# DeltaNet's small products placed side by side in row and column groups of the array

## The chip, the cores and the metric

The kernel runs on one core of one Trainium2 chip, as one program. The metric is the device time of one execution in microseconds (us); less is better. The engines are named as the profile names them: PE is the matrix engine TensorE (PEld its weight loads), DVE is VectorE, ACT is ScalarE, POOL is GpSimd, and SP is the engine whose queue issues the DMAs. All matrix results land in PSUM, in banks of 128 x 512 f32.

## The reference, cut to what matters

One layer of a hybrid encoder block over 1024 positions of 1024 channels: a gated DeltaNet branch (mixer A), a banded attention branch (mixer B), two gates, an output projection, and a feed-forward part with a short convolution. The change touches mixer A alone, and there the following:

```python
h = rmsnorm(x, norm_mix_w)                       # (1024, 1024)
proj = h @ w_in                                  # q, k, v, z, beta logits, decay logits, ...
...
qa = l2norm(qa)                                  # q / sqrt(sum of squares over the 128 channels of a head + EPS)
beta = sigmoid(ba)                               # 4 heads: 4 beta logits and
g = -exp(a_log) * softplus(aa + dt_bias)         # 4 decay logits for every position
# chunks of 64 positions, 4 heads; per chunk and head:
a_mat = beta * (k @ k.T) * dec_strict            # 64 x 64, strictly lower triangular
sol = triangular_solve(a_mat + eye, rhs)         # unit lower triangular
...
oa = rmsnorm(oa, gdn_norm_w) * silu(z)
```

## The kernel before, in words

Positions stand along the free dimension: BH and BL hold the high and the low part of the input (times the norm's weight) as fp32r, 128 channels by 1024 positions in 8 blocks k. A projection of 128 columns over one half (512 positions) is 24 matmuls of 128x512 in proj_half (L118): for each k high by high, high by low, low by high. The row factor of the RMSNorm, rb, is multiplied in afterwards on VectorE (tile u for the convolutions, gt for the gates).

The order of work is the scheduler's: the kernel is written as a program, every instruction has a priority from its place in it, and the scheduler fixes the order on each engine beforehand by a cost model; the engines then run their queues in that order and wait on semaphores. Two things steer it: `tc.high_priority(offset=PRI)` pulls the recurrent part of a head forward, and `behind()` (L54) puts instructions behind the last matmul traced. The lists C1 to APK at the top of the file say after which step of the fill each part of a head starts. The loop at L662 goes over the heads: while the chain of head h runs (gdn_chain, 16 dependent steps), the projections of the heads to come and of the gates fill TensorE.

What the change and the prediction's steps touch:

- first_split (L208) loads the transposed input in four quarters xT (two for each half of the positions, 4 blocks k each) and makes BH and BL of them. The quarters share the buffers of the tag "WQ", of which there are three, with the tiles WQ of the heads.
- first_rms (L224) loads the rows of x and builds rb through a product of ones with a diagonal (psrb).
- ba_half (L285) computes the 8 logits (4 beta, 4 decay) of one half: wba2 holds the 8 columns of the weight as a high and a low part in 16 of 32 columns, and 16 fp32r matmuls (8 blocks by BH and BL) of 32 columns add up in 32 partitions of the tile psba. baf takes them times rb, and decays (L295) turns them with the constant matrix fold, which adds the high and the low part.
- gdn_solve (L520) inverts the 32x32 diagonal blocks on VectorE, stores them (dZ) and loads them into the block diagonal of zt by four DMAs on SP. gdn_apply (L533) then makes the 32x32 block below the diagonal for each 64-position chunk: a transpose on VectorE, a product nL by zt (tile psB1, "psB" in the profile), a copy to B1 on ScalarE, a product with the transposed block (tile psZ21, "psZ"), a copy into zt. This is written for e = 0 and then for e = 1, the two chunks of each of the 8 blocks of 128 positions; e = 0 reads partitions 32 to 63 and writes 0 to 31 in the first product, e = 1 reads 96 to 127 and writes 64 to 95. The products psW and psU, which start the chain, read zt.
- gdn_qnorm (L605) squares q (sqq) and sums over the 128 channels: eight matmuls with sqq as weights (128x128) and a column of ones as the moving operand, handed to proj_half through the list side, one after each k. gdn_qnorm2 (L614) copies the sums to sx by two copies of 64x8, with the two chunks of a block exchanged. gdn_rms (L622) uses sx at L629 (adding EPS and scaling) and L631, for the norm of the head's output.

Of the kernel before, what the change touches and what calls it, by code (L numbers as in the profile page):

```python
# [8 lines left out]
F32 = mybir.dt.float32  # L9
F32R = mybir.dt.float32r  # L10
AF = mybir.ActivationFunctionType
ALU = mybir.AluOpType
# [4 lines left out]
P = 128  # L17
D = 1024
KT = D // P
T = 1024  # L20
NT = T // P
HN = 512
CH = 64
# [23 lines left out]
def hybrid_kernel(ctx: ExitStack, tc: tile.TileContext, a):  # L47
    nc = tc.nc
    last = {}

    def mm(*args, **kw):
        last["mm"] = nc.tensor.matmul(*args, **kw).ins  # L52
# [6 lines left out]
    cst = ctx.enter_context(tc.tile_pool(name="cst", bufs=1))  # L59
# [7 lines left out]
    BH = big.tile([P, KT, T], F32R, name="BH")  # L67
    BL = big.tile([P, KT, T], F32R, name="BL")
# [1 line left out]
    ident = cst.tile([P, P], F32, name="ident")  # L70
    mhalf = cst.tile([P, 16], F32, name="mhalf")
    nc.vector.memset(mhalf, -0.5)
    ones = cst.tile([P, 1], F32, name="ones")
    nc.vector.memset(ones, 1.0)

    def rsqrt(out, in_):
        n = in_.shape[-1]
# [37 lines left out]
    side = []  # L115
# [45 lines left out]
    psc = psy.enter_context(tc.tile_pool(name="psc", bufs=3, space=PSUM))  # L161
# [32 lines left out]
    gp = gx.enter_context(tc.tile_pool(name="gp", bufs=1, reuse_waits="tile"))  # L194
    gc = gx.enter_context(tc.tile_pool(name="gc", bufs=1, reuse_waits="tile"))
    gd = gx.enter_context(tc.tile_pool(name="gd", bufs=2, space=DRAM))


    ones2 = gc.tile([P, P], F32, name="ones2")
# [3 lines left out]
    nw = prm[:, 49:57]  # L203

    rb = cst.tile([P, T], F32, name="rb")
    ws = []

    def first_split(e, step, wk=None):  # L208

        s = slice(e * HN, (e + 1) * HN)  # L210
        for q in range(2):
            xT = gp.tile([P, 4, HN], F32, tag="WQ", name="xT", bufs=3)
            for j in range(4):
                k = 4 * q + j
                if wk and k in wk:
                    first_w(k, wk[k])
                if j % step == 0:
                    nc.sync.dma_start(xT[:, j:j + step, :],
                                      a["xT"][k * P:(k + step) * P, s].rearrange("(k p) t -> p k t", p=P))
                nc.scalar.activation(BH[:, k, s], xT[:, j, :], AF.Copy, scale=nw[:, k:k + 1])  # L220
                nc.vector.scalar_tensor_tensor(out=BL[:, k, s], in0=xT[:, j, :], scalar=nw[:, k:k + 1],  # L221
                                               in1=BH.bitcast(F32)[:, k, s], op0=ALU.mult, op1=ALU.subtract)
# [32 lines left out]
    nc.sync.dma_start(ident, a["consts"][:, 0:P])  # L255
    first_rms(0)
    wba = prm[:, 65:129].rearrange("p (k c) -> p k c", c=8)
    wba2 = gp.tile([P, KT, 32], F32R, tag="mb", name="wba2")
    nc.vector.memset(wba2.bitcast(F32), 0.0)
    nc.vector.tensor_copy(wba2[:, :, 0:8], wba)  # L260
    nc.vector.tensor_tensor(out=wba2[:, :, 8:16], in0=wba, in1=wba2.bitcast(F32)[:, :, 0:8], op=ALU.subtract)
    cw = prm[:, 0:48].rearrange("p (t j) -> p t j", j=4)
    nc.vector.tensor_scalar_mul(prm[:, 0:49], prm[:, 0:49], 0.5)
    gnw = prm[:, 48:49]
# [18 lines left out]
    baf = gp.tile([P, T], F32, tag="zs", name="baf")  # L283

    def ba_half(e):  # L285
        s = slice(e * HN, (e + 1) * HN)
        psb = psc.tile([P, HN], F32, tag="c", name="psba")
        for k in range(KT):
            mm(psb[0:32], wba2[:, k, :], BH[:, k, s], start=k == 0, stop=False)
            mm(psb[0:32], wba2[:, k, :], BL[:, k, s], start=False, stop=k == KT - 1)  # L290
        nc.vector.tensor_mul(baf[0:32, s], psb[0:32], rb[0:32, s])

    fold = gc.tile([32, 8], F32, name="fold")
    nc.sync.dma_start(fold, a["fold"])
    def decays():  # L295
        psg = psa.tile([P, HN], F32, tag="a", name="psbat")
        for p in range(NT):
            mm(psg[:, p * 8:(p + 1) * 8], baf[0:32, p * P:(p + 1) * P], fold, start=True, stop=True)
        bav = psg[:, 0:64].rearrange("p (n c) -> p n c", c=8)

        beta = gc.tile([P, NT, GH], F32, name="beta")
# [231 lines left out]
    def gdn_apply(c):  # L533
        nL, zt = c["nL"], zts[0]
        Z11 = gp.tile([P, NT, 32], F32, tag="Z11", name="Z11")
        psx1 = psa.tile([P, HN], F32, tag="a", name="psB1")
        B1 = gp.tile([P, NT, 32], F32, tag="B1", name="B1")
        psx2 = psa.tile([P, HN], F32, tag="a", name="psZ21")
        for e in range(2):
            r0 = slice(e * CH, e * CH + 32)  # L540
            r1 = slice(e * CH + 32, (e + 1) * CH)
            nc.vector.transpose(out=Z11[r0], in_=zt[r0, :, r0])
            for p in range(NT):
                mm(psx1[r0, p * 32:(p + 1) * 32], nL[r1, p, 0:32], zt[r1, p, r1], start=True, stop=True)
            nc.scalar.copy(B1[r0].rearrange("p n j -> p (n j)"), psx1[r0, 0:256])
            for p in range(NT):
                mm(psx2[r0, p * 32:(p + 1) * 32], Z11[r0, p, :], B1[r0, p, :], start=True, stop=True)
            nc.scalar.copy(zt[r0, :, r1], psx2[r0, 0:256].rearrange("p (n j) -> p n j", j=32))

        WQ, nKs, Vs = c["WQ"], c["nKs"], c["Vs"]  # L550
        U = gp.tile([P, NT, P], F32, tag="U", name="U")
        for q in range(2):
            n = slice(4 * q, 4 * q + 4)
            psW = psa.tile([P, HN], F32, tag="a", name="psW")
            for i in range(4):
                mm(psW[:, i * P:(i + 1) * P], nKs[:, 4 * q + i, :], zt[:, 4 * q + i, :], start=True, stop=True)
            w4 = psW.rearrange("p (n e i) -> p n e i", e=2, i=CH)
            for e in range(2):
                nc.scalar.copy(WQ[:, n, e * 192:e * 192 + CH], w4[:, :, e, :])
            psU = psa.tile([P, HN], F32, tag="a", name="psU")  # L560
            for i in range(4):
                mm(psU[:, i * P:(i + 1) * P], zt[:, 4 * q + i, :], Vs[:, 4 * q + i, :], start=True, stop=True)
            nc.scalar.copy(U[:, n, :], psU.rearrange("p (n d) -> p n d", d=P))
        c["U"] = U
# [40 lines left out]
    def gdn_qnorm(c):  # L605

        sqq = gp.tile([P, NT, P], F32, tag="zs", name="sqq")
        nc.scalar.activation(sqq, c["WQ"][:, :, 64:192], AF.Square)
        psn = psc.tile([P, 8], F32, tag="c", name="psn")
        for p in range(NT):  # L610
            side.append(lambda p=p: mm(psn[:, p:p + 1], sqq[:, p, :], ones, start=True, stop=True))
        c["psn"] = psn

    def gdn_qnorm2(c):  # L614

        psn = c["psn"]
        sx = gp.tile([P, NT], F32, tag="sx", name="sx", bufs=2)
        for e in range(2):
            nc.scalar.copy(sx[(1 - e) * CH:(2 - e) * CH], psn[e * CH:(e + 1) * CH])
        c["sx"] = sx  # L620

    def gdn_rms(c):  # L622
# [39 lines left out]
    for h in range(-1, GH):  # L662
# [35 lines left out]
        n = 0  # L698
# [229 lines left out]
    c = {}  # L928
# [825 lines left out]
def layout(inp):  # L1754
# [6 lines left out]
    def col_tiles(w):  # L1761
# [33 lines left out]
    r["consts"] = np.concatenate(  # L1795
        [np.eye(P), le, le[:, (i + CH) % P], gt, half, ~half, (i % CH)[:, None] <= j[None, :],
         (i % CH)[:, None] > j[None, :], e8], axis=1).astype(np.float32)
    r["fold"] = np.concatenate([np.eye(8), np.eye(8), np.zeros((16, 8))], axis=0).astype(np.float32)
    return r


# [12 lines left out]
```

## Time and profile before

| what | value |
|---|---|
| time, median of 3 runs | 1572.11 us |
| the runs | 1569.9, 1572.11, 1572.12 us |
| span of the profiled execution | 1571.7 us |
| granted TensorE clock, mean | 0.997 |
| PE busy, share of the span | 1520.5 us, 97% |
| PEld busy | 1246.0 us, 79% |
| DVE busy | 1122.3 us, 71% |
| ACT busy | 715.4 us, 46% |
| POOL busy | 597.3 us, 38% |

The span runs from the first to the last instruction of one execution under the profiler; its own time is the span and what little lies around it, and the median of the runs stands 0.4 us above the span. Busy times of an engine add up what it was occupied with; matmuls overlap, so the distance between the starts of two matmuls says more of their cost than their duration. In a row of the timeline the first number is the start in us, the second the time in us of the row, which may cover several instructions (xN), then engine, line, operation, output<-inputs, for matmuls rows*columns of the weights and the shape of the moving operand, and in brackets how long the engine had stood idle and what ended that. Most matmuls come through one helper and bear its line, L52, so they are told apart by tile. In the views of waits the numbers after the colon are us in all, times, and the longest. In the table by stretch the columns are the stretch, its length, busy us and instructions of PE, PEld, DVE, ACT and POOL, the granted clock, and the DMAs' share and GB/s.

### The profile page before, as it was taken

The page shows a single profiled execution, that of the slowest core. Times are in us where ns is not written, and L with a number is a line of the kernel's source. Part 1 is how long each engine was busy: PE and PEld are TensorE (multiplying, and loading weights), DVE is VectorE, ACT ScalarE, POOL GpSimd, SP SyncE. Part 2 cuts the span into 40 slices and gives each one's busy share as a digit, 9 for nine tenths or more (in the row PEclk, how much of TensorE's full clock was granted, in tenths as well). Part 3 has the DMA queues.
Part 4 walks back from the last instruction along what each step waited for, and adds up shares of the span by engine and source line. Part 5 has one row for each costly group of instructions (what it writes and reads, how often), then busy time and mean ns, then how long its engine had stood idle before and what let it go on. Part 6 is the DMA issues. An engine that isn't in the chain of part 4 may idle for free.

```text
span 1571.7 us, 21185 instructions
## 1 busy us (share of the span) xinstructions
PE 1520.5 (97%) x7687; PEld 1246.0 (79%) x7687; DVE 1122.3 (71%) x2146; ACT 715.4 (46%) x1408; POOL 597.3 (38%) x455
## 2 busy tenths in 40 slices
PE   8999999999999999999999999999999999999997
PEld 6778777886777788787887888888888888788875
DVE  7885867948536878866664567777777777786886
ACT  7644526363225656654222345444444443433344
POOL 3522223212131101110220259877777775323253
PEclk9999999999999999999999999999999999999998
DMA  8112131122131101113553213323223232775523
GB/s 297 40 45 88 44 101 31 54 78 68 61 125 49 36 23 57 30 61 119 171 180 109 94 67 107 122 101 101 101 101 101 101 101 98 264 233 162 180 81 141
DMA packets 74505, 162.03 MB, mean 103 GB/s; under 512 B 15649, under 2 KB 16929, under 8 KB 74401
## 3 DMA queue, kind: packets, MB, share of 16 engines
q1 hardware_dynamic: 74400, 160.68, 30.8%
q8 instruction: 60, 0.98, 0.2%
q14 instruction: 45, 0.36, 0.1%
HBM read 120.55 MB, written 40.11 MB: 102 GB/s over the span
## 4 chain that ended last, share of the span: by engine, by line
PE 49%; DVE 3%; issue 2%; DMA 1%; ACT 1%; SPq 1%; POOL 0%; POOLq 0%; DVEq 0%; ACTq 0%
PE psph L52 8%; PE pb L52 7%; PE psd L52 6%; PE psout L52 5%; PE pa L52 5%; PE pc L52 5%; PE pb L1151 4%; PE psd L1506 3%; PE pa L1151 2%; PE pc L1151 2%; DVE wdl L1165 1%; DVE yu L1165 1%; PE pso L52 1%; SPq L1165 1%; DMA araw<-dA 1%
## 5 line engine op out<-in xcount | busy, mean ns | idle before, releaser
L82 POOL TENSOR_TENSOR wlo<-wraw,whi 128x1024 fp32r<-128x1024 f32 (+1 forms) x57 | 120.0, 2106 | 477.8 <-ACT whi L81 288.1
L52 PE MATMUL psph<-BH,whi 128*128 128x512 f32 x688 | 280.7, 408 | 10.5 <-ACT BH L220 5.2
L52 PE MATMUL psph<-BL,whi 128*128 128x512 f32 x688 | 275.6, 401 | 1.2 <-DVE BL L221 1.2
L52 PE MATMUL psph<-BH,wlo 128*128 128x512 f32 x688 | 275.3, 400 | 0.0
L52 PEld LDWEIGHTS psph<-BH,whi 128*128 128x128 f32 x688 | 130.6, 190 | 33.4 <-ACT BH L220 5.4
L1165 POOL TENSOR_TENSOR ol<-wraw,oh 128x512 fp32r<-128x512 f32 x110 | 150.4, 1385 | 6.6 <-ACT oh L1165 6.5
L52 PEld LDWEIGHTS psph<-BL,whi 128*128 128x128 f32 x688 | 130.7, 190 | 22.9 <-DVE BL L221 2.2
L52 PEld LDWEIGHTS psph<-BH,wlo 128*128 128x128 f32 x688 | 130.4, 190 | 22.9
L52 PE MATMUL psd<-wdl,ah 128*128 128x512 f32 (+1 forms) x311 | 121.9, 392 | 5.3 <-DVE wdl L1165 5.3
L1165 POOL TENSOR_TENSOR al<-araw,ah 128x1024 fp32r<-128x1024 f32 (+1 forms) x28 | 68.3, 2441 | 145.8 <-ACT ah L1165 145.7
L52 PE MATMUL psd<-wdh,ah 128*128 128x512 f32 (+1 forms) x311 | 120.2, 390 | 1.5 <-ACT wdh L1165 1.5
L1506 PE MATMUL psd<-wdh,al 128*128 128x512 f32 (+1 forms) x311 | 121.0, 389 | 0.0
L1165 POOL TENSOR_TENSOR wraw<-wraw 128x512 f32<-128x512 f32 x86 | 119.1, 1385 | 4.9
L1165 ACT CAST oh<-wraw 128x512 fp32r<-128x512 f32 x110 | 67.8, 619 | 103.5 <-POOL wraw L1165 103.3
L1165 DVE TENSOR_TENSOR wdl<-W,wdh 128x512 fp32r<-128x512 f32 x77 | 86.6, 1163 | 27.9 <-ACT wdh L1165 27.9
L1165 ACT CAST ah<-araw 128x1024 fp32r<-128x1024 f32 (+1 forms) x39 | 40.6, 1040 | 113.0 <-PE psd L52 57.8
L81 ACT CAST whi<-wraw 128x1024 fp32r<-128x1024 f32 (+2 forms) x61 | 55.3, 907 | 73.0 <-PE psph L52 50.3
L1165 POOL TENSOR_TENSOR gl<-wraw,gh 128x512 fp32r<-128x512 f32 x42 | 56.2, 1340 | 68.6 <-ACT gh L1165 68.6
L52 PEld LDWEIGHTS psd<-wdl,ah 128*128 128x128 f32 x311 | 58.7, 189 | 19.8 <-DVE wdl L1165 8.0
L52 PEld LDWEIGHTS psd<-wdh,ah 128*128 128x128 f32 x311 | 58.8, 189 | 14.1 <-ACT wdh L1165 1.9
L1151 PE MATMUL pa<-BH,gh 128*128 128x512 f32 x176 | 68.6, 390 | 0.0
L52 PE MATMUL pa<-BH,gl 128*128 128x512 f32 x176 | 68.5, 389 | 0.0
(343 smaller groups left out, 3851.0 us busy)
## 6 DMA issues: line engine op xcount, KB each, us to landing
wraw<-w_up SPq DMA_DIRECT2D x44, 512.0 KB, 5.1
wraw<-w_tiles SPq DMA_DIRECT2D x42, 512.0 KB, 3.5
araw<-dA SPq DMA_DIRECT2D x77, 256.0 KB, 3.0
dA<-yu SPq DMA_DIRECT2D x33, 512.0 KB, 3.1
W<-w_down SPq DMA_DIRECT2D x44, 256.0 KB, 4.9
xt<-x SPq DMA_DIRECT2D x16, 512.0 KB, 5.1
dG<-gt SPq DMA_DIRECT2D x16, 512.0 KB, 2.9
ta<-dG SPq DMA_DIRECT2D x16, 256.0 KB, 2.8
```

The costliest lines, as they stand in the source:

```text
L52: last["mm"] = nc.tensor.matmul(*args, **kw).ins
L81: nc.scalar.copy(hi, src)
L82: (eng or nc.gpsimd).tensor_tensor(out=lo, in0=src, in1=hi.bitcast(F32), op=ALU.subtract)
L1151: i = nc.tensor.matmul(ps, wh[:, k], xh[:, k], start=start and k == 0, stop=False, **kw)
L1165: return lambda *args, **kw: tc.keep_in_program_order(f(*args, **kw))
L1506: i = nc.tensor.matmul(ps, al[:, j, ts], wh[:, es], start=False, stop=stop, **kw)
```

## The change

Three groups of small products are placed in different row and column groups of the 128x128 array, and what they need is arranged for it.

- Logits: the 8 blocks k are multiplied in f32 straight from xT, whose quarters are kept in a list (xTs), by the weight times the norm's weight (wba2, f32, 8 of 32 columns used). Block k = 4q + j goes to the 32 partitions j of psba, so four column groups hold four partial sums, over two rounds q. fold is now 128x8 and adds the four.
- Solve: the loops over e and p in gdn_apply are exchanged, so that the products of e = 0 and e = 1, which use different row groups and column groups, alternate; both copies to B1 follow the first 16 products, both copies to zt the second.
- Norm sums: ones (32 columns of ones2) are now the weights and sqq the moving operand, 256 columns for each of four matmuls, each in a column group of its own. All four are handed out at once. gdn_qnorm2 copies the result (tile sn, in the buffer of B1), stores four of its rows to DRAM (dN) and loads sx from there in two DMAs with pieces of one element.

```diff
--- before.py
+++ after.py
@@ -70,8 +70,6 @@
     ident = cst.tile([P, P], F32, name="ident")
     mhalf = cst.tile([P, 16], F32, name="mhalf")
     nc.vector.memset(mhalf, -0.5)
-    ones = cst.tile([P, 1], F32, name="ones")
-    nc.vector.memset(ones, 1.0)
 
     def rsqrt(out, in_):
         n = in_.shape[-1]
@@ -205,11 +203,14 @@
     rb = cst.tile([P, T], F32, name="rb")
     ws = []
 
+    xTs = ([], [])
+
     def first_split(e, step, wk=None):
 
         s = slice(e * HN, (e + 1) * HN)
         for q in range(2):
-            xT = gp.tile([P, 4, HN], F32, tag="WQ", name="xT", bufs=3)
+            xTs[e].append(gp.tile([P, 4, HN], F32, tag="WQ", name="xT", bufs=3))
+            xT = xTs[e][-1]
             for j in range(4):
                 k = 4 * q + j
                 if wk and k in wk:
@@ -255,10 +256,9 @@
     nc.sync.dma_start(ident, a["consts"][:, 0:P])
     first_rms(0)
     wba = prm[:, 65:129].rearrange("p (k c) -> p k c", c=8)
-    wba2 = gp.tile([P, KT, 32], F32R, tag="mb", name="wba2")
-    nc.vector.memset(wba2.bitcast(F32), 0.0)
-    nc.vector.tensor_copy(wba2[:, :, 0:8], wba)
-    nc.vector.tensor_tensor(out=wba2[:, :, 8:16], in0=wba, in1=wba2.bitcast(F32)[:, :, 0:8], op=ALU.subtract)
+    wba2 = gp.tile([P, KT, 32], F32, tag="mb", name="wba2")
+    nc.vector.memset(wba2, 0.0)
+    nc.vector.tensor_tensor(out=wba2[:, :, 0:8], in0=wba, in1=nw.unsqueeze(2).broadcast_to([P, KT, 8]), op=ALU.mult)
     cw = prm[:, 0:48].rearrange("p (t j) -> p t j", j=4)
     nc.vector.tensor_scalar_mul(prm[:, 0:49], prm[:, 0:49], 0.5)
     gnw = prm[:, 48:49]
@@ -285,17 +285,18 @@
     def ba_half(e):
         s = slice(e * HN, (e + 1) * HN)
         psb = psc.tile([P, HN], F32, tag="c", name="psba")
-        for k in range(KT):
-            mm(psb[0:32], wba2[:, k, :], BH[:, k, s], start=k == 0, stop=False)
-            mm(psb[0:32], wba2[:, k, :], BL[:, k, s], start=False, stop=k == KT - 1)
-        nc.vector.tensor_mul(baf[0:32, s], psb[0:32], rb[0:32, s])
-
-    fold = gc.tile([32, 8], F32, name="fold")
+        for q in range(2):
+            for j in range(4):
+                mm(psb[j * 32:(j + 1) * 32], wba2[:, 4 * q + j, :], xTs[e][q][:, j, :], start=q == 0, stop=q == 1,
+                   skip_group_check=True)
+        nc.vector.tensor_mul(baf[:, s], psb, rb[:, s])
+
+    fold = gc.tile([P, 8], F32, name="fold")
     nc.sync.dma_start(fold, a["fold"])
     def decays():
         psg = psa.tile([P, HN], F32, tag="a", name="psbat")
         for p in range(NT):
-            mm(psg[:, p * 8:(p + 1) * 8], baf[0:32, p * P:(p + 1) * P], fold, start=True, stop=True)
+            mm(psg[:, p * 8:(p + 1) * 8], baf[:, p * P:(p + 1) * P], fold, start=True, stop=True)
         bav = psg[:, 0:64].rearrange("p (n c) -> p n c", c=8)
 
         beta = gc.tile([P, NT, GH], F32, name="beta")
@@ -536,15 +537,18 @@
         psx1 = psa.tile([P, HN], F32, tag="a", name="psB1")
         B1 = gp.tile([P, NT, 32], F32, tag="B1", name="B1")
         psx2 = psa.tile([P, HN], F32, tag="a", name="psZ21")
-        for e in range(2):
-            r0 = slice(e * CH, e * CH + 32)
-            r1 = slice(e * CH + 32, (e + 1) * CH)
+        rr = [(slice(e * CH, e * CH + 32), slice(e * CH + 32, (e + 1) * CH)) for e in range(2)]
+        for r0, r1 in rr:
             nc.vector.transpose(out=Z11[r0], in_=zt[r0, :, r0])
-            for p in range(NT):
+        for p in range(NT):
+            for r0, r1 in rr:
                 mm(psx1[r0, p * 32:(p + 1) * 32], nL[r1, p, 0:32], zt[r1, p, r1], start=True, stop=True)
+        for r0, r1 in rr:
             nc.scalar.copy(B1[r0].rearrange("p n j -> p (n j)"), psx1[r0, 0:256])
-            for p in range(NT):
+        for p in range(NT):
+            for r0, r1 in rr:
                 mm(psx2[r0, p * 32:(p + 1) * 32], Z11[r0, p, :], B1[r0, p, :], start=True, stop=True)
+        for r0, r1 in rr:
             nc.scalar.copy(zt[r0, :, r1], psx2[r0, 0:256].rearrange("p (n j) -> p n j", j=32))
 
         WQ, nKs, Vs = c["WQ"], c["nKs"], c["Vs"]
@@ -606,17 +610,26 @@
 
         sqq = gp.tile([P, NT, P], F32, tag="zs", name="sqq")
         nc.scalar.activation(sqq, c["WQ"][:, :, 64:192], AF.Square)
-        psn = psc.tile([P, 8], F32, tag="c", name="psn")
-        for p in range(NT):
-            side.append(lambda p=p: mm(psn[:, p:p + 1], sqq[:, p, :], ones, start=True, stop=True))
+        psn = psc.tile([P, 256], F32, tag="c", name="psn")
+
+        def sums():
+            for j in range(4):
+                mm(psn[j * 32:(j + 1) * 32], ones2[:, 0:32], sqq[:, 2 * j:2 * j + 2, :].rearrange("p n t -> p (n t)"),
+                   start=True, stop=True)
+
+        side.append(sums)
         c["psn"] = psn
 
     def gdn_qnorm2(c):
 
-        psn = c["psn"]
+        sn = gp.tile([P, 256], F32, tag="B1", name="sn")
+        nc.scalar.copy(sn, c["psn"])
+        dN = gd.tile([4, 256], F32, tag="dN", name="dN")
+        nc.sync.dma_start(dN, sn[0:P:32, :])
         sx = gp.tile([P, NT], F32, tag="sx", name="sx", bufs=2)
         for e in range(2):
-            nc.scalar.copy(sx[(1 - e) * CH:(2 - e) * CH], psn[e * CH:(e + 1) * CH])
+            nc.sync.dma_start(sx[(1 - e) * CH:(2 - e) * CH, :],
+                              bass.AP(tensor=dN.tensor, offset=dN.offset + e * CH, ap=[[1, CH], [P, NT]]))
         c["sx"] = sx
 
     def gdn_rms(c):
@@ -1795,7 +1808,7 @@
     r["consts"] = np.concatenate(
         [np.eye(P), le, le[:, (i + CH) % P], gt, half, ~half, (i % CH)[:, None] <= j[None, :],
          (i % CH)[:, None] > j[None, :], e8], axis=1).astype(np.float32)
-    r["fold"] = np.concatenate([np.eye(8), np.eye(8), np.zeros((16, 8))], axis=0).astype(np.float32)
+    r["fold"] = np.tile(np.concatenate([np.eye(8), np.zeros((24, 8))], axis=0), (4, 1)).astype(np.float32)
     return r
 
 
```

## The prediction

> **What bounds the kernel now.** I read the page's busy table first, then the 40 slices, then the idle time of TensorE by releaser in the first 420 us, which hold every line that the change touches, and then the busy time of each engine in stretches of that part.
>
> ```profile
> PE 1520.5 (97%) x7687; PEld 1246.0 (79%) x7687; DVE 1122.3 (71%) x2146; ACT 715.4 (46%) x1408; POOL 597.3 (38%) x455
> ...
> PE   8999999999999999999999999999999999999997
> ...
> PE pss L52 <- DVE U L579: 7.3, 6, 1.6
> PE psph L52 <- ACT BH L220: 5.2, 1, 5.2
> PE psph L52 <- DVE gt L171: 3.1, 3, 1.8
> PE psph L52 <- DVE u L381: 1.0, 1, 1.0
> ...
> 25.00:55.00 30.00, 29.85 (x142) 23.41 (x141) 28.15 (x45) 18.18 (x32) 9.66 (x14) 1.00 0.51 178
> 84.00:125.00 41.00, 37.99 (x173) 30.71 (x172) 37.54 (x87) 12.36 (x20) 8.75 (x8) 1.00 0.20 65
> 125.00:230.00 105.00, 102.74 (x624) 83.31 (x623) 72.72 (x179) 47.59 (x119) 27.79 (x27) 1.00 0.22 67
> ```
>
> TensorE is fed without a break: one start-up wait of 5.2 us, then a handful of waits of 1 to 2 us, nearly all on VectorE. So an instruction taken off TensorE is worth the time by which it holds up its successor, unless VectorE (third pair of columns in the stretches: 28.15 of 30 us, 37.54 of 41, later 72.72 of 105) cannot follow. Busy times are no use for this, because matmuls overlap (a 390 ns matmul starts every 0.23 us). I price by distances between starts, on the timeline of TensorE:
>
> ```profile
> 15.94 0.39 PE L52 MATMUL psba<-BH,wba 128*32 128x512 f32 x1
> ...
> 18.95 0.40 PE L52 MATMUL psba<-BL,wba 128*32 128x512 f32 x1
> ...
> 41.61 0.39 PE L52 MATMUL psph<-BH,whi 128*128 128x512 f32 x1
> ...
> 46.83 0.39 PE L52 MATMUL psph<-BH,wlo 128*128 128x512 f32 x1
> ...
> 73.23 1.10 PE L52 MATMUL psQ<-WQ,kf 128*64 128x64 f32 x32
> 74.26 0.50 PE L52 MATMUL psph<-BH,whi 128*128 128x512 f32 x1
> ...
> 102.68 0.39 PE L52 MATMUL psph<-BH,wlo 128*128 128x512 f32 x1
> 102.90 0.28 PE L52 MATMUL psn<-ones,sqq 128*128 128x1 f32 x2
> ...
> 103.59 0.39 PE L52 MATMUL psph<-BH,wlo 128*128 128x512 f32 x1
> ...
> 130.34 0.39 PE L52 MATMUL psph<-BH,wlo 128*128 128x512 f32 x1
> 130.66 0.69 PE L52 MATMUL psB<-zt,nL 32*32 32x32 f32 x16
> 131.27 0.50 PE L52 MATMUL psph<-BH,whi 128*128 128x512 f32 x1
> 131.61 0.40 PE L52 MATMUL psph<-BL,whi 128*128 128x512 f32 x1
> ...
> 132.57 0.21 PE L52 MATMUL psB<-zt,nL 32*32 32x32 f32 x1
> 132.60 0.19 PE L52 MATMUL psZ<-B,Z 32*32 32x32 f32 x1
> 132.62 0.19 PE L52 MATMUL psB<-zt,nL 32*32 32x32 f32 x1
> 132.63 0.19 PE L52 MATMUL psZ<-B,Z 32*32 32x32 f32 x1
> 132.66 0.19 PE L52 MATMUL psB<-zt,nL 32*32 32x32 f32 x1
> ...
> 135.03 0.40 PE L52 MATMUL psph<-BL,whi 128*128 128x512 f32 x1
> 135.27 0.39 PE L52 MATMUL psph<-BH,wlo 128*128 128x512 f32 x1
> 135.49 1.05 PE L52 MATMUL psW<-zt,nKs 128*128 128x128 f32 x8
> 136.38 0.83 PE L52 MATMUL psU<-Vs,zt 128*128 128x128 f32 x6
> ```
>
> A plain projection matmul costs (46.83 - 41.61) / 23 steps = 0.227 us, one of the logits (18.95 - 15.94) / 13 = 0.232. An f32 matmul is two instructions in the trace. With 128 columns each instruction takes (136.38 - 135.49) / 8 = 0.111. The psQ products sit in two column groups of the array by turns and go at (74.26 - 73.23) / 32 = 0.032 with 64-column weights and 64 moving columns, where half of 0.111 would be 0.056: two groups already run side by side. The 32x32 products of one group go at (131.27 - 130.66) / 16 = 0.038; where psB and psZ, in different row and column groups, happen to alternate, four steps take 132.66 - 132.57 = 0.09, so 0.022 each at most. Going into such a burst costs 0.32 - 0.23 = 0.09 over a plain start and coming out 0.34 - 0.23 = 0.11: 0.2 a burst.
>
> **The change part by part.** *Logits.* Before, 32 matmuls at 0.232: 7.4 us, 3.7 a half. After, each half has 8 f32 matmuls over 512 columns, two for each of four column groups. No row shows an f32 matmul that wide. The bounds for one instruction are 0.227 (the 512-column row) and 4 x 0.111 = 0.444 (psW scaled); I take 0.444, the row of the same type. Side by side, a group has 4 instructions: 4 x 0.444 + 0.2 = 2.0 a half, a gain of 1.7. One after another it would be 16 x 0.444 + 0.2 = 7.3, a loss of 3.6 a half. With 0.227 and side by side it would be 1.1, a gain of 2.6. I take side by side, by psQ. But in the first half some of the 8 may be strewn singly between projections, as its first logits are now, and each then costs 0.9 alone; I count 0.9 for that half: 0.9 + 1.7 = 2.6. The sum over the four groups rides on the fold product, whose weights still have 128 columns: nothing. Splitting wba into two parts becomes one multiplication, 0.2 us of VectorE less. The baf product has 128 lanes in place of 32 with the same 512 columns: nothing.
>
> *xT kept longer.* The fourth xT quarter takes the buffer of the first, and its loads now wait for the first round of logits as well as for ScalarE and VectorE.
>
> ```profile
> 17.20 2.31 SPq L218 DMA_DIRECT2D xT<-xT  x4
> 21.33 10.86 SPq L231 DMA_DIRECT2D xt<-x  x4
> ...
> 30.70 1.05 ACT L233 ACTIVATE xt<-xt 128x1024 f32<-128x1024 f32 x1
> ```
>
> The queue comes to these loads only at 17.2 + 2 x 0.58 = 18.4. The first round, from 15.9 on, ends by about 16.9: 1.5 us of cover. Behind them on SP stand the x rows of the second half, the constants, fold and the weights; the x rows are first read at 30.70, so a few us more would still be covered. Nothing.
>
> *Norm sums.* Before, a group of three projections with a psn takes 103.59 - 102.68 = 0.91, so psn costs 0.91 - 3 x 0.227 = 0.23, eight times: 1.84 a head. After, four matmuls over 256 columns in four column groups: 2 x 0.222 + 0.2 = 0.64, a gain of 1.2 a head, 4.8 in all. One after another it is 8 x 0.222 + 0.2 = 2.0, a loss of 0.15 a head; at half the price a gain of 1.4. I take 1.2 on the same ground. Then the sums go through memory: one ScalarE copy of 256 columns in place of two small ones, one store, two loads of 4-byte pieces, all on SP.
>
> ```profile
> L619 ACT COPY sx<-psn x8: 157/160/163, 110.8 to 398.0; 64x8 f32<-64x8 f32 x8
> L548 ACT COPY zt<-psZ x8: 362/362/363, 132.9 to 407.1; 32x256 f32<-32x256 f32 x8
> ...
> dZ<-Zt SPq DMA_DIRECT2D x4, 128.0 KB, 1.7
> zt<-dZ SPq DMA_DIRECT2D x16, 32.0 KB, 2.1
> ...
> DVE Z L542 <- DMA zt<-dZ: 15.7, 7, 4.7
> SPq L87 <- POOL wlo L82: 207.5, 19, 24.8
> ```
>
> The copy is 0.36 for 0.32. The nearest transfer is the solve's own trip, 1.7 and then 2.1 us; the 4-byte loads can hardly be quicker and may be several us slower. Their reader is the EPS step on VectorE (L629), which the scheduler puts into VectorE's order as soon as it believes sx there (L629 follows L619 at once), with solve steps, conv taps and gate products of projections behind it. When VectorE waits for zt in the same way (15.7 us in 7 waits, 4.7 at most), TensorE has its two projection banks, 24 x 0.227 = 5.4 us each, and none of its waits listed above is put down to zt. I count nothing; without that cover it would be about 2.2 us a head, 9 in all. SP waits for each store to land before the next load goes; weights queued behind have a second buffer.
>
> *Solve blocks.* From 130.34 to 135.03 a head starts 8 projection matmuls (131.85, 133.19, 133.52, 133.75 and 134.70 lie between the quoted ones) and both blocks: 4.69 - 8 x 0.227 = 2.87. After, two bursts of 32 instructions at 0.018 to 0.022, say 0.6, plus 0.2: 1.6. Gain 1.3 a head, 5.2 in all; without overlap between groups 2 x (32 x 0.038 + 0.2) = 2.8 and a gain of nothing. psZ now waits for two copies of 0.36 on ScalarE in place of one; projections of 0.227 stand ready to fill in.
>
> **The sum.** 2.6 + 4.8 + 5.2 = 12.6 us less on TensorE. VectorE takes part of it back: logits and head 0's sums (3.8) fall ahead of the stretch 84 to 125, where VectorE is busy 92% and TensorE already waits for gt and u; I give up half, 1.9. Of the other 8.8, won where VectorE is busy 70%, a tenth: 0.9. Left: 9.8. The profiled execution has a span of 1571.7 us; the runs' median is 1572.1, so what lies around the span is 0.4. 1572.1 - 9.8 = 1562.
>
> **A rule against it.** The TensorE time of psQ says that weight loads of two column groups are hidden too: 0.032 a step is less than 0.056, though both groups use all rows. The Trainium skill (TensorE: Matmul & The Clock Gate, Part 3, The mechanism) has it that a weight load overlaps running matmuls only where the row groups differ. The trace disagrees with this for psQ, as far as 64-column loads show; the logits and the norm sums use all rows as well. That is rival B.
>
> **The rivals.** *B: weight loads of groups that share rows are not hidden.* 32 columns cost 0.111 / 4 = 0.028; 32 loads for the logits and 32 for the norm sums are 1.8 us: 1564. Against it stands psQ.
>
> *C: wide f32 operands do not run side by side*, since each group streams 512 or 256 columns of its own from 128 rows, which no row shows. Logits -7.3, norm sums -0.6, solve +4.7: 1572.1 + 3.2 = 1575. For it: psQ streams only 64 columns and proves two groups, not four. It decides against the change once the groups run less than about 1.5 side by side.
>
> *D: VectorE is the bound*, and the freed time returns as waits for gt, u, U and S. If all of the first 3.8 and half of the 8.8 goes, and waits for sx take 2 more, 2.4 are left: 1570. For it: 92% in 84 to 125. Against: VectorE itself waits for TensorE elsewhere.
>
> *E: slower, by sx.* If its loads queue on SP behind a weight load that waits for POOL (207.5 / 19 = 10.9 us on average), VectorE stands at L629 that long, TensorE outlasts 5.4 of it, and four heads lose 4 x 5.5 = 22: 1572.1 - 9.8 + 22 = 1584. It decides from 5.4 + 9.8 / 4 = 7.9 us a head. Against: zt goes through the same queue with 4.7 at most.
>
> **How the numbers follow.** Forecast 0.62, B 0.07, C 0.08, D 0.16, E 0.07. What can be told from no change is 0.2%, 3.1 us. Faster: the forecast, B and a quarter of D, 0.73. Same: the rest of D and some of C, 0.14. Slower: E and most of C, 0.13. The range starts at 1555 (forecast with 0.227 an instruction, 1.8 more on the logits and 0.8 on the sums, and nothing given back to VectorE, 2.8, with a little for a shorter chain) and ends at 1571 with D inside; C and E stay out.
>
> **What would show it.** Logits: 8 f32 matmuls a half in about 2 us; 7 us is C. psn: starts of four matmuls nearly together, some 0.6 a head. psB and psZ: 32 instructions in 0.6 and no second pair of bursts. L629: a wait on sx under 5 us. TensorE's waits for VectorE before 130 us: up by 2 us, not by 4. Wrong it would be through C's single file, through a wait on sx of 8 us or more, or through a new order of instructions that moves waits elsewhere.

## The result, and the profile after

The changed kernel takes 1589.58 us (median of 4 runs, 1587.73 to 1593.38) against 1571.01 us before (4 runs, 1569.78 to 1572.12) on the same chip: a ratio of 1.0115, 95% interval 1.0102 to 1.0129. It is 18.6 us slower; the forecast was 10 us faster. The profiled execution has a span of 1591.6 us (time 1593.4), with a mean granted clock of 0.990, where the execution before showed 0.997. Of all runs below one stands apart: a run of logits_solve took 1886.3 us at a mean clock of 0.751, and is left out of its ratio.

The three edits do on TensorE what the forecast said. The lines are rows of its timeline after: the logits of the second half, one head's norm sums, and (from the run with the solve alone, because both bursts are whole there) the solve's blocks:

```profile
35.84 0.40 PE L52 MATMUL psph<-BH,wlo 128*128 128x512 f32 x1
36.16 1.92 PE L52 MATMUL psba<-xT,wba 128*32 128x512 f32 x14
38.01 0.50 PE L52 MATMUL psph<-BH,whi 128*128 128x512 f32 x1
...
112.69 0.39 PE L52 MATMUL psph<-BH,wlo 128*128 128x512 f32 x1
113.01 0.64 PE L52 MATMUL psn<-sqq,ones 128*32 128x256 f32 x8
113.58 0.50 PE L52 MATMUL psph<-BH,whi 128*128 128x512 f32 x1
```

```profile
133.33 0.69 PE L52 MATMUL psB<-zt,nL 32*32 32x32 f32 x32
133.95 0.50 PE L52 MATMUL psph<-BH,whi 128*128 128x512 f32 x1
...
134.84 0.71 PE L52 MATMUL psZ<-B,Z 32*32 32x32 f32 x32
135.49 0.50 PE L52 MATMUL psph<-BH,whi 128*128 128x512 f32 x1
...
136.52 0.72 PE L52 MATMUL psW<-zt,nKs 128*128 128x128 f32 x5
```

From the projection ahead to the projection behind, less one plain start of 0.227, the logits take 38.01 - 35.84 - 0.23 = 1.94 us (3.7 before), the norm sums 113.58 - 112.69 - 0.23 = 0.66 (1.84 before). A head's solve goes from its first psB to psW in 136.52 - 133.33 = 3.19, where it was 135.49 - 130.66 = 4.83; but 9 projection matmuls started in between before and 7 do now. Without them it is 4.83 - 9 x 0.227 = 2.79 and 3.19 - 7 x 0.227 = 1.60, a gain of 1.2. That is 1.8 + 4 x 1.18 + 4 x 1.2 = 11 us gone from TensorE's own work (the first half's logits come in split bursts and are left out of this sum). The loss is elsewhere, in two places.

The first is VectorE's work in head 0. Busy time by stretch (PE, PEld, DVE, ACT, POOL; the row "sum" covers 60 to 130 us), first before, then after:

```profile
82.00:90.00 8.00, 8.00 (x37) 6.47 (x35) 4.35 (x6) 4.58 (x11) 2.77 (x3) 1.00 0.23 70
...
sum 70.00, PE 65.60 PEld 53.63 DVE 56.48 ACT 34.11 POOL 25.69; mean PE 21.87 PEld 17.88 DVE 18.83 ACT 11.37 POOL 8.56
```

```profile
82.00:90.00 8.00, 8.00 (x37) 6.61 (x36) 0.35 (x2) 7.82 (x23) 0.00 (x0) 1.00 0.31 82
...
sum 70.00, PE 59.95 PEld 48.39 DVE 48.65 ACT 32.62 POOL 22.87; mean PE 19.98 PEld 16.13 DVE 16.22 ACT 10.87 POOL 7.62
```

and the waits in this part of the kernel, first VectorE's for Lr before, then those of VectorE and TensorE after (us in all, times, longest):

```profile
DVE tmp L516 <- DMA Lr<-dL: 0.9, 1, 0.9
```

```profile
DVE u L382 <- PE psph L52: 7.8, 3, 4.2
DVE tmp L517 <- DMA Lr<-dL: 6.9, 1, 6.9
...
PE psph L52 <- DVE u L382: 7.4, 1, 7.4
...
PE psdec L52 <- issue: 1.8, 1, 1.8
```

VectorE stands 6.9 us at the first solve step (L517, L516 before) until Lr has landed, with conv taps queued behind it; between 82 and 90 us it works 0.35 us, and from 60 to 130 us it does 48.65 us of work instead of 56.48. Then TensorE stands 7.4 us for u. The longest such wait before was 1.0 for u.

The second place is where nothing was edited. Two rows of TensorE's timeline in the last stage, 33 starts apart before and 31 after:

```profile
1439.67 0.39 PE L52 MATMUL psd<-wdh,ah 128*128 128x512 f32 x1
...
1447.15 0.39 PE L52 MATMUL psd<-wdh,ah 128*128 128x512 f32 x1
```

```profile
1439.81 0.40 PE L52 MATMUL psd<-wdl,ah 128*128 128x512 f32 x1
...
1447.05 0.39 PE L1519 MATMUL psd<-wdh,al 128*128 128x512 f32 x1
```

The same matmul starts every 7.48 / 33 = 0.227 us before and every 7.24 / 31 = 0.234 after, at a granted clock of 1.0 in both.

### The profile page after: what moved, and what is told of

It reads as the page before. It is cut to its first block, busy times and chain, and to the rows that moved or that the text cites. A ratio compares the mean times of both kernels' runs of the same rounds, so it can differ in the third digit from the quotient of the medians.

```text
span 1591.6 us, 21137 instructions
## 1 busy us (share of the span) xinstructions
PE 1532.5 (96%) x7655; PEld 1238.7 (78%) x7655; DVE 1136.8 (71%) x2144; ACT 712.7 (45%) x1404; POOL 597.2 (38%) x455
## 4 chain that ended last, share of the span: by engine, by line
PE 49%; DVE 4%; issue 2%; DMA 1%; ACT 1%; SPq 1%; POOL 0%; POOLq 0%; DVEq 0%; ACTq 0%
PE psph L52 8%; PE pb L52 7%; PE psd L52 6%; PE psout L52 5%; PE pa L52 5%; PE pc L52 5%; PE pb L1164 4%; PE psd L1519 3%; PE pc L1164 2%; PE pa L1164 2%; DVE wdl L1178 1%; DVE yu L1178 1%; SPq L1178 1%; PE pso L52 1%; DMA araw<-dA 1%
## 5 line engine op out<-in xcount | busy, mean ns | idle before, releaser
L1178 POOL TENSOR_TENSOR ol<-wraw,oh 128x512 fp32r<-128x512 f32 x110 | 157.8, 1451 | 6.6 <-ACT oh L1178 6.5
L1178 POOL TENSOR_TENSOR wraw<-wraw 128x512 f32<-128x512 f32 x86 | 111.9, 1302 | 4.9
L1519 PEld LDWEIGHTS psd<-wdh,al 128*128 128x128 f32 x311 | 58.7, 189 | 13.8
```

The lines of the kernel that those rows point to most:

```text
L1178: return lambda *args, **kw: tc.keep_in_program_order(f(*args, **kw))
L1519: i = nc.tensor.matmul(ps, al[:, j, ts], wh[:, es], start=False, stop=stop, **kw)
```

## Experiments on the late stages: 32 bytes

The change deletes the tile `ones` ([128, 1] f32, for which 32 bytes of every partition are set aside). Everything that is allocated after it from the left side of SBUF moves down by 32 bytes; tiles on the right side (the transposed states XT1 to XT3, the weights wdh and wdl) stay. The psd matmuls above read the weights wdh and wdl, from the right, and ah or al, from the left. My theory A was that operands which then lie differently make matmuls slow; rival O was that only order, clock and transfers differ. Three runs keep the order of all engines and move bytes. Each was timed beside the kernel before, 1571.6 us.

**pad_back**: the changed kernel and

```diff
+    ones = cst.tile([P, 1], F32, name="ones")
+    nc.vector.memset(ones, 1.0)
```

> The changed kernel with the 32-byte tile `ones` allocated and set again, read by nobody. Order of instructions on every engine as in the changed kernel. Theory A (addresses): without that tile everything allocated from the left lies 32 bytes lower, tiles on the right side don't, and matmuls whose two operands then differ by 32 modulo 64 start every 233 to 235 ns instead of 227. The lag of the changed kernel grows from 5.5 us at 460 us to 19.9 at the end, 14 us; with the tile back these 14 go and the 5.5 stay: 1575 to 1578. Rival O (order, clock, transfers alone): 32 bytes nobody reads change nothing: 1588 to 1593.

Measured: 1576.56 us, ratio to before 1.0026 (1.0014 to 1.0039). That is 4.9 us above before, where the changed kernel stood 18.6 above: 13.7 us are gone with a tile that nobody reads.

**before_less32**: the kernel before and

```diff
-    ones = cst.tile([P, 1], F32, name="ones")
-    nc.vector.memset(ones, 1.0)
...
-            side.append(lambda p=p: mm(psn[:, p:p + 1], sqq[:, p, :], ones, start=True, stop=True))
+            side.append(lambda p=p: mm(psn[:, p:p + 1], sqq[:, p, :], ones2[:, 0:1], start=True, stop=True))
```

> The kernel before with only the tile `ones` gone: the norm sums read the first column of ones2 instead. Order on every engine as before. Theory A: the operands lie as in the changed kernel, so about 14 us slower: 1583 to 1587, and the matmuls psd from 233 ns apart. Rival O: 1570 to 1573.

Measured: 1584.05 us, ratio 1.008 (1.0068 to 1.0092): 12.4 us slower with no other change.

**right_shift**: the changed kernel and

```diff
+    rpad = ctx.enter_context(tc.tile_pool(name="rpad", bufs=1, side="right"))
+    spare = rpad.tile([P, 1], F32, name="spare")
+    nc.vector.memset(spare, 1.0)
```

> The changed kernel without the tile `ones`, but with a 32-byte tile at the start of the right side, so that right tiles move by 32 as well and all large operands lie at 0 modulo 64 (32 modulo 64 before). Theory A in its relative form (what counts is whether the two operands lie alike): as with the tile back, 1575 to 1578. Theory A in its absolute form (operands at 0 modulo 64 are slow): no gain or a loss, 1589 to 1600. Rival O: 1588 to 1593.

Measured: 1576.03 us, ratio 1.0029 (1.0018 to 1.0039). The same rows as above in this run, 33 starts:

```profile
1439.68 0.39 PE L52 MATMUL psd<-wdl,ah 128*128 128x512 f32 x1
...
1447.16 0.39 PE L52 MATMUL psd<-wdl,ah 128*128 128x512 f32 x1
```

0.227 again. With the left side 32 bytes lower and the right side too, these matmuls lose nothing, and the time is that of pad_back: what counts is how tiles lie to each other and not where they lie. Rival O and the absolute form are out. Two later runs (beside 1572.7 and 1572.2 us for before) asked for the period.

**before_less64**: before_less32 and `mhalf = cst.tile([P, 8], ...)` in place of `[P, 16]`, 64 bytes in all.

> The kernel before without `ones`, as in the run that came to 1584.1, and with mhalf 8 columns wide in place of 16, so that the left side lies 64 bytes lower and both operands are alike modulo 64 again; the order of all engines is as there. Theory A, relative modulo 64: 1570 to 1573. Rival (any shift of the left side against the right counts, or its exact distance): 1580 to 1586.

Measured: 1579.41 us, ratio 1.004 (1.0028 to 1.0053). A miss: 64 bytes are not neutral. The psd rows, 32 starts:

```profile
1439.70 0.39 PE L52 MATMUL psd<-wdl,ah 128*128 128x512 f32 x1
...
1447.03 0.39 PE L52 MATMUL psd<-wdh,ah 128*128 128x512 f32 x1
```

0.229, between 0.227 and 0.234.

**before_less128**:

```diff
-    sml = ctx.enter_context(tc.tile_pool(name="sml", bufs=8))
+    sml = ctx.enter_context(tc.tile_pool(name="sml", bufs=7))
+    spare = sml.tile([P, 1], F32, tag="spare", name="spare", bufs=1)
+    nc.vector.memset(spare, 1.0)
```

> The kernel before with one buffer less for each of the five small tiles of its pool sml and one spare 32-byte tile, so that BH, BL, oh and ol lie 128 bytes lower and the weights whi and the right side stay; order of all engines as before. A period of 64 is out since 64 bytes cost 6.7 us. With a period of 128: 1570 to 1573, and pc and pb of the feed-forward stage 227 ns apart. With one of 256 or more: 1575 or more, and these matmuls 229 to 235 ns apart.

Measured: 1586.61 us, ratio 1.0092 (1.008 to 1.0104). In the feed-forward stage of this run BH and oh both moved, XT1h did not:

```profile
1000.72 0.39 PE L52 MATMUL pc<-BH,ol 128*128 128x512 f32 x1
...
1002.76 0.40 PE L52 MATMUL pc<-BH,ol 128*128 128x512 f32 x1
...
1005.79 0.39 PE L1153 MATMUL pc<-XT1h,oh 128*128 128x512 f32 x1
...
1008.10 0.39 PE L52 MATMUL pc<-XT1l,oh 128*128 128x512 f32 x1
```

9 starts in 2.04, 0.227, where both moved; 10 in 2.31, 0.231, where one did. So distances of 32, 64 and 128 bytes from the old one cost time. The period is none of these; what it is stays open.

The two operands of the slow matmul itself don't explain every row, though. In the same run another product of BH and oh, for which both moved as well, is slow:

```profile
991.91 0.40 PE L1153 MATMUL pb<-BH,oh 128*128 128x512 f32 x1
...
994.45 0.40 PE L52 MATMUL pb<-BH,ol 128*128 128x512 f32 x1
```

11 starts in 2.54, 0.231. And in before_less32, where both moved by 32 bytes, the pc of BH and oh go from 997.48 to 1000.01, 11 starts at 0.230, where they went at 0.227 before. That the shift of 32 bytes costs the time is shown; which accesses get into each other's way is not, and the mechanism inside the chip stays open.

## Experiments on the parts

With the tile kept, each part of the diff alone, then in pairs (1571.6 us before for the first, 1572.1 for the others).

> The kernel before with the solve's 32x32 blocks alone put side by side; addresses as before. Prediction's term: 1.3 us a head, 5.2 in all, less a tenth: 1566 to 1567. Rival (the two later copies on ScalarE hold TensorE up, or the new order costs head 0 time): 1570 or more.

**solve_only**: 1567.63 us, ratio 0.9972 (0.9962 to 0.9982): 4.0 us faster, 4.7 forecast.

> The kernel before with the queries' norm sums alone in four column groups and their way through memory; addresses as before. Prediction's term: 1.2 us a head, 4.8 in all, less what VectorE takes back: 1567 to 1568. With the tile back the whole change stands 4.9 us above before and the solve alone 4.0 below, so 9 us are lost in logits and sums. Theory S (the sums' two extra transfers a head, in the queue ahead of the solve's rows Lr, or the order that they bring, cost head 0 its time): 1576 to 1581. Theory L (the logits' order does): 1566 to 1569.

**sums_only**: 1571.76 us, 1.0004 (0.9996 to 1.0013): nothing, 4.8 forecast. Neither the forecast nor theory S.

> The kernel before with the logits alone in four column groups, from xT in f32; addresses as before. Prediction's term: 2.6 us less, half of it given back: 1570. Theory L: the earlier logits change the order of ScalarE's and VectorE's work up to 100 us, TensorE stands still and its clock is halved after: 1575 to 1581. Theory S: 1569 to 1572.

**logits_only**: 1579.18 us, 1.0049 (1.0037 to 1.0061): 7.1 us slower. Theory L.

> Solve and norm sums, logits as before; addresses as before. If the parts add up and theory L holds, 1571.6 - 4.0 - 4 or so = 1562 to 1565. Under theory S 1572 to 1577.

**solve_sums**: 1567.05 us, 0.997 (0.9958 to 0.9982): 5.1 us faster, and faster than both kernels of this case. It is the lowest median of all the kernels run, but its interval and that of solve_only (0.9962 to 0.9982) overlap almost wholly: the two can't be told apart.

> Logits and solve, norm sums as before; addresses as before. If the parts add up and theory S holds, 1571.6 - 4.0 - 1 = 1565 to 1568. Under theory L 1571 to 1577.

**logits_solve**: 1574.22 us, 1.0011 (1.0003 to 1.002): theory L; 7.1 - 4.0 = 3.1 above before was to be expected from the parts, 2.1 measured (1.7 by the ratio).

By the medians the parts add up to -4.0 - 0.4 + 7.1 = 2.7 us, and the whole with the tile kept stands 4.9 above before. By the ratios it is -4.4 + 0.6 + 7.7 = 3.9 against 4.1. So no interaction between the parts is shown.

## Experiments on the logits

The run with logits alone shows the picture of the changed kernel:

```profile
82.00:90.00 8.00, 8.00 (x37) 6.64 (x36) 1.04 (x3) 7.82 (x23) 0.19 (x1) 1.00 0.31 82
...
sum 70.00, PE 61.00 PEld 49.94 DVE 51.03 ACT 33.88 POOL 22.84; mean PE 20.33 PEld 16.65 DVE 17.01 ACT 11.29 POOL 7.61
```

psbat, which ends the logits, is 1.6 us earlier than before. But the scheduler now orders ScalarE otherwise: the squares for ssk end at 75.3 instead of 67.3 us, between other work; bv on GpSimd follows, the 32 scalings (Kd, Vs, nKs) that wait for it end at 89.4 instead of 84.6, and conv copies and tanh stand behind them. VectorE's first solve step comes ahead of the conv taps and waits 5.0 us for Lr.

**lg_sq** wrote ScalarE's order out (all_sqe: the same on the whole change, with one small Exp behind the Ln):

```diff
+                last["sq"] = nc.scalar.activation(jk, nKs[:, 4 * e + i, :], AF.Square, ...).ins
...
+            with behind("sq"):
                 nc.scalar.copy(Vs[:, 4 * e:4 * e + 4, :], ...)
...
+        if w is None and "sq" in last and ti == GH + 1:
+            with behind("sq"):
+                w = load_w(a["w_tiles"][ti])
```

> The logits alone, as before this run (1579.2 against 1572.1), with ScalarE's order in head 0 written out: copies of psv, decb, decT and head 1's first weight cast are issued behind the eight squares (ssk). In the kernel with logits alone these squares end at 75.1 us, before at 67.1; bv follows, then the scalings, and TensorE stands 5.5 us at 98.8. Theory O (the logits do their work, and lose by the order that they bring to ScalarE): the squares end by 70, the wait shrinks to under 2.5 us, 1570 to 1575. Rival W (the wide f32 matmuls or the xT held longer cost it, with any order): 1577 to 1580.

> The whole change with the 32-byte tile back (1576.6), with ScalarE's order in head 0 written out as above, and with one small Exp behind the Ln so that the table of Exp and Tanh is loaded there and not in front of eg. If solve and sums bring 5.1 as measured and the logits 1 to 2.6 once the order is right: 1564 to 1567. If the logits lose by something else than this order: 1572 to 1577.

Measured: 1590.02 us, 1.0109 (1.0095 to 1.0123), and 1583.43 us, 1.0071 (1.0058 to 1.0083), beside 1572.7. The squares end at 65.4, and it is slower. TensorE's waits in lg_sq up to 130 us:

```profile
PE psdec L52 <- issue: 7.0, 1, 7.0
...
PE psph L52 <- ACT whi L81: 4.5, 1, 4.5
PE psph L52 <- POOL wlo L82: 4.1, 1, 4.1
```

I had moved the wrong cast: whi of head 1's first projection is what TensorE works on from 51 us on, and it now stood behind the squares. The run says nothing of theory O; it says that TensorE stands 15.6 us in these three waits with the cast 18 us late (65.3 instead of 46.8 in logits_only, where the wait before psdec is 1.8 and the other two are missing).

**lg_warm** fills the wait of logits_only at 93 to 98.8 us with 19 matmuls that nobody reads:

```diff
+            if h < 0 and n == 4:
+                with behind():
+                    keep_warm(19)   # mm(f, BH[:, 0, 0:P], BH[:, i % KT, 0:HN]) into a free bank
```

> The logits alone, with 19 matmuls that nobody reads (4.3 us) put into TensorE's wait of 5.5 us at 93 to 98.8; the order of the rest up to there is as in the kernel with logits alone (1579.2). Theory K (part of the loss is the clock granted after a wait: 0.50 for some 6.8 us behind this one, half of that time lost, 3.4 us): 1575 to 1577, and no halved clock at 96 to 102. Rival: the halved clock is only a sign of the wait and covers no time of its own: 1578 to 1580.

Measured: 1579.14 us, 1.0038 (1.0024 to 1.0052). The stretches 93 to 99 in logits_only, then in lg_warm:

```profile
93.00:96.00 3.00, 0.38 (x2) 0.00 (x0) 3.00 (x5) 0.08 (x1) 1.59 (x1) 0.92 0.13 22
96.00:99.00 3.00, 0.17 (x1) 0.17 (x1) 3.00 (x9) 1.31 (x3) 0.78 (x2) 0.50 0.41 156
```

```profile
93.00:96.00 3.00, 3.00 (x15) 2.49 (x14) 3.00 (x5) 0.00 (x0) 1.55 (x1) 1.00 0.15 35
96.00:99.00 3.00, 1.69 (x9) 1.08 (x7) 3.00 (x11) 1.27 (x3) 0.78 (x2) 1.00 0.36 142
```

The clock is 1.00 where it was 0.50, and the time is the same within the intervals (logits_only 1.0037 to 1.0061), above theory K's range. The intervals alone would leave room for K's 3.4 us; the profiles say more: the first psB of head 0 starts at 137.1 us with the filling and at 137.3 without. VectorE is busy 3.00 of 3.00 us in both. In this stretch VectorE sets the pace, and a slow TensorE hides behind it. The half clock that both runs have between 60 and 79 us was not tested.

**lg_p2, all_p2** pin only the copies to Vs and the cast of head 1's third projection; **all_p2e** adds an Exp behind the Ln:

```diff
-        if w is None and "sq" in last and ti == GH + 1:
+        if w is None and "sq" in last and ti in (2 * GH + 1,):
...
+        with tc.high_priority(offset=PRI), behind("ln"):
+            nc.scalar.activation(jk0[:, 0:1], ident[:, 0:1], AF.Exp)
```

> The logits alone (1579.2), with ScalarE's order in head 0 written out once more: only the copies of psv, decb, decT and the cast of the weights of head 1's third projection are issued behind the eight squares; the first two casts stay where they were. ScalarE's and VectorE's order from eg to the scalings then is nearly the one of the kernel before, with the conv taps ahead of the first solve step. Theory O (order): the wait of 5.5 us at 98.8 falls below 2, 1570 to 1575. Rival W (the wide f32 logits or the xT held longer cost time by themselves): 1577 to 1581.

> The whole change with the 32-byte tile back (1576.6) and the same order written out. Theory O: solve and sums bring 5.1, the logits 0 to 2.6: 1564 to 1569. Rival W: 1574 to 1578.

> As the kernel before this in the list, with one small Exp behind the Ln, so that the 1.28 us load of the table stands there and not in front of eg, where everything on ScalarE waits. If that load was on the path: 1 us less than without it, 1563 to 1568. If not: the same.

Measured beside 1572.2: 1577.78 us, 1.0036 (1.0024 to 1.0048); 1571.43 us, 0.9996 (0.9987 to 1.0004); 1571.48 us, 0.9995 (0.9986 to 1.0004). In lg_p2 the wait for u is gone and another stands in its place, the cast now behind the scalings:

```profile
PE psph L52 <- ACT whi L81: 7.1, 1, 7.1
...
DVE kf L401 <- ACT th L396: 10.3, 1, 10.3
```

The early table load brings nothing. lg_p2 ends in the range of rival W, all_p2 between the two ranges that were given for it: the wait came back elsewhere, so these two decide nothing between O and W.

**lg_z0, all_z0** take the priority from head 0's scalings, whose results are first read behind 130 us:

```diff
-        with behind("exp"):
+        with tc.high_priority(offset=-PRI if h == 0 else 0), behind("exp"):
             for p in range(NT):
```

> The logits alone (1579.2), and the 32 scalings of head 0 on ScalarE (Kd, Vs, nKs, some 15 us, first read after 130 us) without the high priority, so that conv copies, tanh and weight casts stand between them; VectorE's first solve step then follows the conv taps, and the cast for the third projection stays at 69 us. Theory O (the loss is a wait of 5.5 to 7.1 us at 92 to 99 that an order makes, and the clock after it): no wait over 2 us there, 1569 to 1574. Rival W (the logits' matmuls or xT): 1577 to 1581.

> The whole change with the 32-byte tile back (1576.6) and head 0's scalings without the high priority. Theory O: 1562 to 1568, below solve and sums alone (1567.1) if the logits bring anything. Rival W: 1574 to 1578.

Measured beside 1573.6: 1576.20 us, 1.0017 (1.0007 to 1.0028), and 1570.06 us, 0.9981 (0.9971 to 0.999). The stretches of lg_z0:

```profile
82.00:90.00 8.00, 8.00 (x37) 6.64 (x36) 6.08 (x16) 6.91 (x17) 0.99 (x2) 1.00 0.17 67
...
sum 70.00, PE 66.28 PEld 53.94 DVE 53.78 ACT 33.79 POOL 24.58; mean PE 22.09 PEld 17.98 DVE 17.93 ACT 11.26 POOL 8.19
```

VectorE works 6.08 us between 82 and 90, TensorE 66.28 of 70, and in this profile the first psB starts 2.2 us ahead of before: the forecast's gain on the logits. In time the loss falls from 7.1 to 2.6 us (1.0049 to 1.0017). So most of it was the order, and theory O holds for 4.5 us; both runs end between the ranges of O and W. The last 2.6 go with the granted clock: the three runs of lg_z0 with a mean clock of 0.997 took 1573.4 to 1573.8 us, as long as before, and the two at 0.992 took 1579.7 and 1580.1. Its profile has 3.4 us of half clock at 306 and again at 743 us, which before's has not, and ends level with before (both spans 1571.7). What gain the logits bring under another order is not shown: the 2.2 us at the first psB never reached the median.

## Why the prediction was wrong

- *Local terms: right.* 1.94 a half for the logits (2.0 taken), 0.66 a head for the norm sums (0.64), 1.2 gained a head on the solve (1.3). The groups run side by side: rival C is out, and for these bursts rival B as well. The page TensorE: Matmul & The Clock Gate of the Trainium skill (Part 3, The mechanism), by which weight loads that share row groups are not hidden, would by the prediction's 0.028 a load ask for 8 x 0.028 = 0.22 us more in each burst of norm sums. The trace disagrees: the burst measures 0.66, 0.02 above the sum without them.
- *"xT kept longer": nothing*, right: psbat is 3 us ahead of before (49.53 against 52.59; 1.6 in logits_only). *sx through memory*: right as well; rival E's place was wrong. All four EPS steps, and the landing of sx:

```profile
L642 DVE TENSOR_SCALAR sx<-sx x4: 162/166/2297, 123.3 to 418.9; 128x8 f32<-128x8 f32 x4
...
DMA to landing us min/median/max: 2.4/2.4/2.5
```

  VectorE lists no wait for sx at all. The one step of 2.30 us (from 215.51) runs beside GpSimd's cast of wlo (from 215.40, 2.38 us). That is no cost of sx: the kernel before has the same on a solve step (L516 at 111.09, 2.31 us, beside a cast from 110.84), so VectorE's busy time holds some 2 us for such a cast in both kernels. What E described, VectorE at a DMA with the taps behind it, happened at L517 with Lr, a line that the change does not touch.
- *"VectorE takes back 1.9": the step that failed.* I treated the stretch 84 to 125 as a share to be given back. But VectorE is the bound there (92% before), and earlier logits gave every engine a new order: VectorE lost 7.8 us of work by 130 us, TensorE's waits for VectorE up to there rose from 4.4 to 9.2 us, and head 0 came out 7.1 us late at its first psB (137.74 against 130.66) instead of 2.6 + 1.2 - 1.9 = 1.9 early. With the tile kept and the logits alone it is 6.7 late, and with the scalings' priority taken as well 2.2 early: the order makes the difference. Rival D had the place right, VectorE's waits, but it gave back no more than was won. My last sentence named "a new order of instructions that moves waits elsewhere" and gave it no price and no chance of its own.
- *"VectorE gives back a tenth of 8.8": the solve kept 4.0 of 5.2; the sums, 4.8 in the forecast, brought 0.4 alone and 1.1 beside the solve, neither clear of noise.* Where those 4 us went is open: the profile of sums_only is level with before at the first psB (130.8), 2.5 us ahead at the last one (402.9 against 405.4), and 0.6 ahead at the end, with nothing edited in between. It has half clock at 55 to 59 and 117 to 120 us, which before's profile has not. But the clock does not hide the 4 us: the six runs of sums_only at a mean clock of 0.998 or more took 1569.9 to 1571.2 us, the three of before beside them 1569.9 to 1572.2.
- *Not in the sum at all*: that deleting a 32-byte tile moves everything allocated after it from the left. 13.7 us of the 18.6 come from it, by pad_back; without it the forecast of 1562 would still have been some 15 us too low.

## What to carry to other kernels

Before timing an edit that deletes or adds a tile, hold every other tile where it was; compare the distance between matmul starts in a stage that the edit does not touch, for that shows a shifted layout at once. On a kernel whose order a scheduler makes, price an edit that frees time ahead of a stretch where another engine is the bound by what the new order may do to that engine, and test each part alone: here the solve gained 4.0 us, the sums about nothing, and the logits cost 7.1. A wait removed by pinning an order comes back at the next thing that the pin delays, so look at the list of waits again and not at the wait that was meant.

## What the runs showed of the hardware

*Operands' places.* fp32r matmuls of 128x512 start every 0.227 us, or every 0.229 to 0.234, by how the tiles lie to each other in SBUF: 0, 32, 64 and 128 bytes from the old distance between left and right gave 0.227, 0.234, 0.229 (psd) and 0.231 (pc) in the rows above. The clock is 1.0 in all of them. The pb rows of before_less128 (0.231) show that the distance between a matmul's own two operands is not the whole of it.

*The clock in steps.* Stretches of 3.41 us in logits_only:

```profile
57.98:61.40 3.42, 2.86 (x13) 2.05 (x11) 2.82 (x9) 2.24 (x5) 0.17 (x1) 1.00 0.00 0
61.40:64.81 3.41, 2.20 (x19) 2.23 (x20) 3.13 (x8) 2.17 (x7) 2.12 (x4) 1.00 0.00 0
64.81:68.22 3.41, 3.41 (x9) 2.66 (x9) 0.80 (x2) 2.74 (x8) 1.56 (x2) 0.50 0.00 0
...
71.64:75.05 3.41, 1.64 (x27) 1.19 (x29) 2.22 (x2) 1.84 (x8) 2.16 (x3) 1.00 0.33 113
75.05:78.46 3.41, 3.41 (x51) 3.10 (x48) 2.26 (x4) 0.99 (x5) 3.11 (x4) 0.50 0.12 46
```

Here a stretch with 2.20 or 1.64 us of work on TensorE is followed by one at half clock; one with 2.86 is not. But the busy time that the profile lists does not decide it. In the kernel before, a step of 3.41 us with 1.63 us of work is followed by full clock (the first two lines); in sums_only one listed as busy throughout, 1.9 us of it with psbat's products of 8 columns, is followed by half clock (the last two):

```profile
532.07:535.49 3.42, 1.63 (x10) 1.09 (x9) 3.36 (x6) 1.29 (x4) 1.39 (x1) 1.00 0.29 65
535.49:538.90 3.41, 3.41 (x20) 2.91 (x21) 3.24 (x13) 2.35 (x7) 0.00 (x0) 1.00 0.42 126
...
51.96:55.37 3.41, 3.41 (x24) 3.11 (x24) 2.64 (x4) 0.72 (x2) 0.10 (x1) 1.00 0.52 159
55.37:58.79 3.42, 3.42 (x10) 2.68 (x9) 2.91 (x11) 3.21 (x5) 0.00 (x0) 0.50 0.00 0
```

What counts as work stays open. The Trainium skill (TensorE: Matmul & The Clock Gate, Part 1, What's actually happening) has a free-running window of 3413 ns, and the steps here fit it; but it asks for an idle window of some 3.4 us before the clock falls, and here TensorE worked for 2.20 and 1.64 us of the window. The mean clock differs between executions of one kernel, and the time with it: the 12 runs of pad_back spread from 1571.6 (mean clock 0.994) to 1580.3 us (0.990), the 22 of the kernel before beside them from 1569.9 (0.998) to 1576.1 (0.996). A mean clock 0.001 lower is 3.1 us more at half clock, so at most 1.6 us of TensorE's work (an estimate from the steps of 0.50 above and the span).
